# Sigmoid's table behind the last square root, and projections in the first two attention slots

## The chip, the cores and the metric

The kernel runs on one core of one Trainium2 chip. The metric is the device time of one execution in microseconds (us); the time of a kernel is the median over its runs. TensorE is called PE here, ScalarE ACT, VectorE DVE, GpSimd POOL and SyncE SP, as in the profile.

## The reference

One decoder layer over 1024 tokens of width 1024, in float32, with 16 learned meta tokens ahead of them:

```python
h = h + 0.5 * swiglu(rms_norm(h, ffn1_norm), ffn1_w_in, ffn1_w_out)
u = rms_norm(h, mix_norm) @ w_in                   # one combined projection
hq, hf, hi, hg, sq, sk, sv = split(u)
o_hg = hgrn2(hq, hf, hi, hg, lb, hgrn_out_norm)    # 4 heads, gated linear recurrence in chunks of 128
o_sb = stick_breaking(sq, sk, sv, q_norm, k_norm)  # 8 heads of 64, strictly causal
h = h + concat([o_hg, o_sb]) @ w_out
h = h + 0.5 * swiglu(rms_norm(h, ffn2_norm), ffn2_w_in, ffn2_w_out)
```

Stick breaking: `z = q.k / 8`, `A[t,s] = sigmoid(z_ts) * prod_{s<j<t} (1 - sigmoid(z_tj))`. The product over j is a running product along the keys of a row. In HGRN2 `f = lb + (1 - lb) * sigmoid(hf)`, `k = (1 - lb) * sigmoid(-hf)`, `q = silu(hq)`, and the gate is `silu(hg)`.

## The kernel before, in words

Every float32 product on PE is made of three products of rounded halves (`wh`, `wl`, `xh`, `xl`), the three lines L249 to L251 of `product`. The layer is staged: first feed-forward block (0 to about 735 us of the trace), the entry of the mixer, the attention, the four HGRN heads woven with the first half of the output product, the second half of that product, second feed-forward block. The change touches the entry and the attention.

**The entry.** `sb_project` makes keys, values and queries of two stick-breaking heads at a time (four pairs, p = 0 to 3), and two generators turn them: `sb_qk` transposes queries and keys, sums their squares into `sbs`, takes the square root of the sums on ACT (L1475), the reciprocal on DVE (L1476), scales on POOL (L1479), transposes back, and splits into halves `ohi` and `olo` that are stored. `weave` sets the order of the steps. ACT's functions come from tables: Sqrt has one, Sigmoid another, and an `ACT_TABLE_LOAD` stands where the table changes. Behind the four pairs the entry makes the first 16 pieces of the HGRN columns.

**HGRN columns.** `hgrn_fill` gives 96 pieces: 4 heads of columns v, f, q, g, each cut into two or four spans of tokens, each span into two pieces of 12 matmuls. A span is summed in one PSUM bank (`proj`); its second piece ends with the evacuation (`use`). For f these are two Sigmoids on ACT (L1141, L1142) and two DVE instructions, for q and g a Sigmoid (L1149) and a DVE product that reads the bank again (L1150). Results pass four staging tiles `st` and go to DRAM (`hg_v`, `hg_f`, `hg_k`, `hg_q`, `hg_g`). Column weights come by DMA into `raw`, are rounded by ACT (`wh`, L232) and subtracted by DVE (`wl`, L234).

**The attention.** `sb_jobs` yields 32 jobs: 8 heads, each with four pairs of query blocks (b0 = 0, 6, 2, 4). A job has scores (L1640 and L1641 on PE into one of two `z` buffers; L1642 `keep` and L1643 `sig`, two Sigmoids on ACT; L1646, the running product on DVE; L1653 on POOL), turns (transposes on PE, called `flip`, into one of two buffers; L1618 on ACT and L1619 on DVE make `wu` or, for the meta tokens, `wm`), and values (L1570 and L1572 on PE into `oacc`). `braid` sets the order on PE. It goes slot by slot; job i has its scores in slot i, its turns from slot i + 2 on, and its values from slot i + 3 on (`turn` = 2.0, `value` = 3.0). Each slot is owed 1.22 times its attention's time in projection pieces, which are spread evenly over the slot:

```python
owed += share * sum(t for _, t, _ in now)
while owed > 0:
    step = next(fill, None)
```

So slots 0 and 1, which hold scores alone, are owed little. In the attention only one bank serves the projections, since the other holds the constant `begin`; a new span therefore waits until ACT and DVE have emptied the bank. The other engines' rows follow the order in which the steps are written and the schedule of the recording layer.

**Behind the attention.** `hgrn_attend` loads a head's vT, KB, QA, F, KM and FM from DRAM (L1199, on SP's queue) and makes transposes of vT (`flip<-ident,vT`, L1495), the products within a chunk (`lvl`, L1235), and then seven levels (`lvl`, L1270, with the DVE products L1257 and the copies L1278). The loads of heads 0 to 2 are written behind the attention, as their tiles lie where its keys and queries lay. The projection pieces that `braid` has left over are woven with the first steps of the heads. Then follow the 64 steps of `first_half_of_o`, whose matmuls are called `wo`: they need `wh` and `wl` of the output weights (L222) and `oT`, the attention's result from DRAM (L2240), and all of these stand behind the head loads on SP's queue.

Of the kernel before, what the change touches and what calls it, by code (L numbers as in the profile page):

```python
# [15 lines left out]
AF = mybir.ActivationFunctionType  # L16
# [32 lines left out]
class Block:  # L49
# [1401 lines left out]
    def sb_qk(self, p, qT, kT, pool, mix, dst):  # L1451

        nc = self.nc
        ss, other = (
            pool.tile([P, 65], F32, tag=x, name=x, bufs=2) for x in ("sbs", "sbo")
        )  # L1460
        nat = pool.tile([P, 65, 32], F32, tag="nat", name="nat", bufs=2)
        rows = [(qT, 0, 0, 16), (qT, 512, 16, 16), (kT, 0, 32, 16), (kT, 512, 48, 17)]
        for src, c0, b0, nb in rows:
            y = nat[:, b0 : b0 + nb]
            nc.vector.transpose(y.rearrange("p b d -> p (b d)"), src[:, c0 : c0 + 32 * nb])
            sq = pool.tile([P, 17, 32], F32, tag="sq4", name="sq4", bufs=2)[:, :nb]
            nc.scalar.activation(sq, y, AF.Square)
            nc.vector.tensor_reduce(ss[:, b0 : b0 + nb], sq, mybir.AxisListType.X, ALU.add)
            yield 0, 1500
        for b in range(4):  # L1470
            nc.scalar.copy(
                other[32 * b : 32 * b + 32], ss[32 * (b ^ 1) : 32 * (b ^ 1) + 32]
            )
        nc.vector.tensor_add(ss, ss, other)
        nc.scalar.activation(ss, ss, AF.Sqrt, bias=self.eps, scale=1.0 / 64)  # L1475
        nc.vector.reciprocal(ss, ss)  # L1476
        for _, _, b0, nb in rows:
            y = nat[:, b0 : b0 + nb]
            nc.gpsimd.tensor_mul(  # L1479
                y, y, ss[:, b0 : b0 + nb].unsqueeze(2).broadcast_to([P, nb, 32])  # L1480
            )
        yield 0, 6000
        for src, c0, b0, nb in rows:
            t = src[:, c0 : c0 + 32 * nb]
            nc.vector.transpose(t, nat[:, b0 : b0 + nb].rearrange("p b d -> p (b d)"))
            n = min(32 * nb, (SEQ if src is qT else T) - c0)
            gain, to = (self.qg8, dst[0]) if src is qT else (self.kg, dst[1])
            with self.tc.issue_after(self.rounds[self.columns[-1]]) if p == 3 else ExitStack():
                self.put_split(to, p, slice(c0, c0 + n), t[:, :n], mix, gain)
            yield 0, 1500  # L1490
# [203 lines left out]
    def braid(self, jobs, fill, share, turn, value):  # L1694


        waiting = []
        owed = 0.0
        at = 0
        while True:  # L1700
            job = next(jobs, None)
            for lag, steps in zip((0.0, turn, value), job or ()):
                total, done = sum(t for t, _ in steps), 0.0
                for t, f in steps:
                    waiting.append((at + lag + (done + t / 2) / total, t, f))
                    done += t
            if not waiting:
                break
            now = [x for x in waiting if x[0] < at + 1]
            waiting = [x for x in waiting if x[0] >= at + 1]  # L1710
            owed += share * sum(t for _, t, _ in now)
            more = []
            while owed > 0:
                step = next(fill, None)
                if step is None:
                    break
                more.append(step)
                owed -= step[0]
            now += [(at + (i + 0.5) / len(more), t, f) for i, (t, f) in enumerate(more)]
            for _, _, f in sorted(now, key=lambda x: x[0]):  # L1720
                f()
            at += 1
# [669 lines left out]
```

## Time and profile before

| what | us |
| --- | --- |
| runs: median (lowest to highest of 3) | 1957.84 (1956.85 to 1957.93) |
| the profiled execution: its device time | 1959.65 |
| the profiled execution: its span | 1957.9 |
| PE busy / ACT busy / DVE busy / POOL busy | 1919.8 / 849.6 / 1390.4 / 450.5 |

The span is what the profile's windows and rows are counted from; the device time holds 1.75 us more around it. A row of the timeline gives start, length, engine, line, operation and, in brackets, how long the engine stood idle before it and who released it. PE is busy for 98% of the span, so the 38 us in which it is not are what a change of order can win or lose.

### The profile page before, as it was taken

Reading aid. Unit: us, or ns where it says so; the run is one execution under the profiler, and the core shown is the slowest. Engines: PE = TensorE matmul, PEld = TensorE weight load, DVE = VectorE, ACT = ScalarE, POOL = GpSimd, SP = SyncE. Lnnn points to the kernel's source line nnn. Section 1 sums busy time; section 2 is a strip of 40 time slices with the busy share of each in tenths; the row PEclk is TensorE's granted clock in tenths of the full one; section 3 lists DMA queues with packets and bytes.
Section 4 is the critical chain, followed back from the end, with each engine's and each line's share of the span. In section 5 each row is a group of like instructions: output and inputs, shape, how many; then the busy total and the mean of one; then the engine's idle time right before and its main releaser. Section 6 shows DMA issues by size and latency. Waiting matters only on the chain.

```text
span 1957.9 us, 30218 instructions
## 1 busy us (share of the span) xinstructions
PE 1919.8 (98%) x10607; PEld 1616.6 (83%) x10607; DVE 1390.4 (71%) x2184; ACT 849.6 (43%) x1711; POOL 450.5 (23%) x625
## 2 busy tenths in 40 slices
PE   7999999999999999999999999999999999999999
PEld 6888888788888888888898978887888888888887
DVE  7977877877678665467777766677567767766774
ACT  6523443334444544356666635433232332344443
POOL 3010100001000003133333332210544645530000
PEclk9999999999999999999999999999999999999999
DMA  7356887758965315865454177655634444469473
GB/s 213 93 165 170 253 272 243 233 203 291 375 221 188 127 54 144 193 170 148 128 148 121 57 253 225 161 208 183 198 115 140 128 131 121 132 243 318 154 231 113
DMA packets 381687, 355.54 MB, mean 182 GB/s; under 512 B 129040, under 2 KB 284560, under 8 KB 381536
## 3 DMA queue, kind: packets, MB, share of 16 engines
q1 hardware_dynamic: 359728, 288.98, 48.7%
q0 software_dynamic: 20768, 64.63, 9.5%
q8 instruction: 84, 1.38, 0.3%
q14 instruction: 67, 0.55, 0.1%
q10 hardware_dynamic: 1040, 0.00, 0.0%
HBM read 237.95 MB, written 115.57 MB: 181 GB/s over the span
## 4 chain that ended last, share of the span: by engine, by line
PE 89%; DVE 4%; DMA 3%; ACT 2%; issue 1%; POOL 1%; SPq 1%; DVEq 0%; ACTq 0%; POOLq 0%
PE o L732 21%; PE qb L450 18%; PE qa L450 12%; PE qc L450 12%; PE proj L249 5%; PE proj L251 4%; PE proj L250 4%; PE flip L1495 2%; PE wo L250 1%; PE wo L249 1%; PE wo L251 1%; PE mq L1001 1%; PE oacc L1572 1%; PE oacc L1570 1%; DMA oT<-oD 1%
## 5 line engine op out<-in xcount | busy, mean ns | idle before, releaser
L450 PE MATMUL qb<-T,wh 128*128 128x512 f32 x1056 | 344.6, 390 | 1.3 <-ACT T L309 0.8
L450 PEld LDWEIGHTS qb<-T,wh 128*128 128x128 f32 x1056 | 198.1, 188 | 46.4 <-issue 2.5
L450 PE MATMUL qa<-B,wh 128*128 128x512 f32 x696 | 226.7, 390 | 0.3 <-ACT B L835 0.2
L249 PE MATMUL proj<-xh,wh 128*128 128x512 f32 (+2 forms) x640 | 213.2, 333 | 2.6 <-ACT st L1142 1.3
L732 PE MATMUL o<-t,w 128*128 128x512 f32 x924 | 211.8, 390 | 0.7 <-DVE u L543 0.7
L251 PE MATMUL proj<-xl,wh 128*128 128x512 f32 (+2 forms) x640 | 210.2, 328 | 0.8 <-DVE xl L1957 0.8
L250 PE MATMUL proj<-xh,wl 128*128 128x512 f32 (+2 forms) x640 | 210.1, 328 | 0.0
L732 PE MATMUL o<-parts 128*128 128x512 f32 x924 | 209.6, 389 | 0.0
L450 PE MATMUL qb<-T,wl 128*128 128x512 f32 x528 | 205.5, 389 | 0.0
L732 PEld LDWEIGHTS o<-t,w 128*128 128x128 f32 x924 | 172.8, 188 | 37.8 <-ACT sgm L981 1.1
L732 PEld LDWEIGHTS o<-parts 128*128 128x128 f32 x924 | 173.5, 188 | 36.0
L362 DVE TENSOR_TENSOR wl<-s,wh 128x512 fp32r<-128x512 f32 x160 | 165.6, 1035 | 50.8 <-ACT wh L360 49.9
L360 ACT CAST wh<-s 128x512 fp32r<-128x512 f32 x160 | 99.2, 622 | 188.5 <-PE qb L450 141.1
L450 PEld LDWEIGHTS qa<-B,wh 128*128 128x128 f32 x696 | 130.5, 188 | 28.0 <-DVE B L836 0.5
L360 ACT CAST wh<-raw 128x512 fp32r<-128x512 f32 x120 | 74.4, 621 | 155.8 <-PE qc L450 111.4
L450 PE MATMUL qa<-B,wl 128*128 128x512 f32 x348 | 135.4, 389 | 0.0
L249 PEld LDWEIGHTS proj<-xh,wh 128*128 128x128 f32 x640 | 120.8, 189 | 15.0 <-ACT st L1142 2.2
L251 PEld LDWEIGHTS proj<-xl,wh 128*128 128x128 f32 x640 | 120.7, 189 | 12.3 <-DVE xl L1957 1.2
L250 PEld LDWEIGHTS proj<-xh,wl 128*128 128x128 f32 x640 | 120.8, 189 | 10.1
L450 PE MATMUL qc<-B,wh 128*128 128x512 f32 x352 | 115.1, 390 | 2.3 <-DVE u L543 2.3
L450 PE MATMUL qc<-T,wh 128*128 128x512 f32 x352 | 117.0, 394 | 0.0
L450 PEld LDWEIGHTS qb<-T,wl 128*128 128x128 f32 x528 | 99.1, 188 | 20.2
(393 smaller groups left out, 3819.4 us busy)
## 6 DMA issues: line engine op xcount, KB each, us to landing
raw<-in_ffn_w_in_dram SPq DMA_DIRECT2D x176, 256.0 KB, 4.0
raw<-in_ffn_w_out_dram SPq DMA_DIRECT2D x112, 256.0 KB, 4.5
w2in<-both SPq DMA_DIRECT2D x28, 512.0 KB, 3.4
raw<-in_w_in_dram SPq DMA_DIRECT2D x25, 512.0 KB, 5.2
ks<-kD SPq DMA_DIRECT2D x32, 260.0 KB, 4.8
wout<-both SPq DMA_DIRECT2D x16, 512.0 KB, 3.7
wh<-w2in SPq DMA_DIRECT2D x27, 256.0 KB, 3.1
wl<-w2in SPq DMA_DIRECT2D x27, 256.0 KB, 3.1
```

Of the source, the lines that this page charges most:

```text
L249: nc.tensor.matmul(ps, wh[:, s], xs, start=k == 0, stop=False)
L250: nc.tensor.matmul(ps, wl[:, s], xs, start=False, stop=False)
L251: nc.tensor.matmul(ps, wh[:, s], xl[:, k, c0 : c0 + n], start=False, stop=k == nk - 1)
L360: nc.scalar.copy(hi, src)
L362: self.block_lo = nc.vector.tensor_sub(lo, src, hi.bitcast(F32))
L450: nc.tensor.matmul(ps, a[:, k, :], b[:, k, :], start=start and k == 0 and i == 0, stop=k == 3 and i == 2, skip_group_check=True,)
L732: nc.tensor.matmul(banks[bank][m], y[:, m * P : (m + 1) * P], z, start=start and at == 0 and e == 0, stop=q == nq - 1 and e == 2, skip_gro ...
L1001: nc.tensor.matmul(ps[at : at + 32, :], self.xm[:, 4 * h + k, :], got[i, h][:, k, :], start=h == 0 and k == 0, stop=h == 1 and k == 3, til ...
L1495: self.nc.tensor.transpose(ps[:m, j, :], src[:, s0 : s0 + m], self.ident)
L1570: nc.tensor.matmul(o[:, c], vj, w[0], start=j == 0, stop=False, skip_group_check=True)
L1572: nc.tensor.matmul(o[:64, c], vj[:, :64], w[1], start=False, stop=end, skip_group_check=True)
```

## The change

In `sb_qk` of the last pair (p = 3) a Sigmoid of one column is issued right behind the square root; its result goes into `other` (`sbo` in the rows), which is no longer read. ACT thus loads Sigmoid's table there. In `braid`, slots below `turn` (0 and 1) are also owed the projections for the turns and values of their own jobs, which run in later slots.

```diff
-        nc.scalar.activation(ss, ss, AF.Sqrt, bias=self.eps, scale=1.0 / 64)
+        root = nc.scalar.activation(ss, ss, AF.Sqrt, bias=self.eps, scale=1.0 / 64)
+        if p == 3:
+            with self.tc.issue_after(root.ins):
+                nc.scalar.activation(other[:, :1], self.eps, AF.Sigmoid)
         nc.vector.reciprocal(ss, ss)
...
             owed += share * sum(t for _, t, _ in now)
+            if at < turn:
+                owed += share * sum(t for steps in job[1:] for t, _ in steps)
```

Lines behind the first edit move by 3, behind the second by 5. Counted from the planner's own numbers, slots 0 and 1 get 1 and 0 pieces before and 1 and 3 after; over the attention it is 74 pieces before, with 6 left for the first steps of the HGRN heads, and 76 after, with 4 left. The number of pieces, loads and stores is the same in all; one ACT instruction is added, and no table load.

On ACT, at the end of the entry (`+` and `-` as the difference shows them; `ohi` and `kT` belong to `sb_qk` of the last pair, `st` to the HGRN columns):

```order
 L1475 ACTIVATE sbs<-sbs,eps 128x65
+L1478 ACT_TABLE_LOAD
+L1478 ACTIVATE sbo<-eps 128x1
 L1416 ACTIVATE ohi<-qT,qg_82 128x512
 L1135 COPY st<-proj 128x256
...
 L1416 ACTIVATE ohi<-kT,kg 128x528
 L232 CAST wh<-raw 128x1024
-L1141 ACT_TABLE_LOAD
 L1141 ACTIVATE st<-proj 128x264
 L1142 ACTIVATE st<-proj 128x264
```

The load stood between the rounding of a weight and the first Sigmoid of a column f; it now stands behind the square root.

On PE, slot 1 of the attention before (the scores of the second job, in buffers `z`):

```order
L1640 MATMUL z<-ks,qs 128x456
L1641 MATMUL z<-ks,qs 128x456
...
L1640 MATMUL z<-ks,qs 128x344
L1641 MATMUL z<-ks,qs 128x344
L1640 MATMUL z<-ks,qs 128x348
L1641 MATMUL z<-ks,qs 128x348
```

and after, where each `proj` row of the three is one of four such threes in a piece:

```order
L1643 MATMUL z<-ks,qs 128x456
L1644 MATMUL z<-ks,qs 128x456
L249 MATMUL proj<-xh,wh 128x512
L250 MATMUL proj<-xh,wl 128x512
L251 MATMUL proj<-xl,wh 128x512
...
L1643 MATMUL z<-ks,qs 128x344
L1644 MATMUL z<-ks,qs 128x344
L1643 MATMUL z<-ks,qs 128x348
L1644 MATMUL z<-ks,qs 128x348
```

Three pieces have come between the scores of slot 1: behind the first 456 columns, behind the second, and behind the first 348. From there to the end of the attention the projections are ahead of where they stood by two to five pieces.

On PE, behind the attention before (four pieces of `proj` stand ahead of these rows; `proj` rows stand for the first of 12):

```order
L1495 MATMUL flip<-ident,vT 16x128
L1495 MATMUL flip<-ident,vT 128x128 x8
L249 MATMUL proj<-xh,wh 128x512
...
L1235 MATMUL lvl<-QA,KB 128x128 x8
L1495 MATMUL flip<-ident,vT 16x128
L1495 MATMUL flip<-ident,vT 128x128 x8
L249 MATMUL proj<-xh,wh 128x512
...
L1270 MATMUL lvl<-QA,KP 128x2x64 x4
L1235 MATMUL lvl<-QA,KB 128x128 x8
L1270 MATMUL lvl<-QA,KP 128x2x64 x4
```

and after, again behind four pieces:

```order
L1498 MATMUL flip<-ident,vT 16x128
L1498 MATMUL flip<-ident,vT 128x128 x8
L1498 MATMUL flip<-ident,vT 16x128
L1498 MATMUL flip<-ident,vT 128x128 x8
L1235 MATMUL lvl<-QA,KB 128x128 x16
L1270 MATMUL lvl<-QA,KP 128x2x64 x4
L249 MATMUL wo<-oT,wh 128x512
...
L1498 MATMUL flip<-ident,vT 16x128
L1498 MATMUL flip<-ident,vT 128x128 x8
L1270 MATMUL lvl<-QA,KP 128x2x64 x4
```

Two pieces are gone from here, and the first `wo` step now comes ahead of the third head's transposes and of two levels that preceded it. On SP the head loads, the last store and the loads of `wh`, `wl` and `oT` keep their order.

## The prediction

> **What bounds the kernel now.** I read the page first: engines, then the chain that ended last; then the windows of the attention (860 to 1140) and of the HGRN start (1140 to 1260).
>
> ```profile
> PE 1919.8 (98%) x10607; PEld 1616.6 (83%) x10607; DVE 1390.4 (71%) x2184; ACT 849.6 (43%) x1711; POOL 450.5 (23%) x625
> PE 89%; DVE 4%; DMA 3%; ACT 2%; issue 1%; POOL 1%; SPq 1%; DVEq 0%; ACTq 0%; POOLq 0%
> 860.00:1140.00 280.00, 270.99 (x1865) 244.43 (x1864) 205.11 (x356) 181.21 (x464) 98.86 (x141) 0.99 0.44 124
> 1140.00:1260.00 120.00, 113.02 (x736) 96.68 (x734) 82.05 (x152) 55.01 (x134) 37.62 (x73) 1.00 0.78 237
> ```
>
> PE bounds it. The change adds and removes no matmul, so its effect is PE's idle time and slow time, of which these two windows hold 9.0 and 7.0 us. The clock column (the third from the end: 0.99) says that some of the first was not idle but slow; finer windows find it:
>
> ```profile
> 867.00:868.00 1.00, 1.00 (x5) 0.95 (x5) 1.00 (x2) 1.00 (x5) 0.38 (x1) 0.63 1.00 207
> 868.00:869.00 1.00, 1.00 (x4) 0.71 (x4) 0.89 (x2) 0.74 (x3) 1.00 (x1) 0.50 1.07 237
> 869.00:870.00 1.00, 1.00 (x4) 0.81 (x3) 0.89 (x2) 0.00 (x0) 0.52 (x2) 0.50 0.94 184
> 870.00:871.00 1.00, 1.00 (x5) 0.76 (x4) 1.00 (x3) 0.00 (x0) 0.53 (x1) 0.66 1.21 230
> ```
>
> From 867.4 to 870.7 PE ran at half its clock: 0.37 + 0.5 + 0.5 + 0.34 = 1.7 us lost, behind four us of scattered scores.
>
> **Part 1, the table.** On ACT, then PE and SP:
>
> ```profile
> 844.47 0.72 ACT L1416 ACTIVATE ohi<-qT,qg 128x512 fp32r<-128x512 f32 x1 [2.58 <-DVE qT L1485]
> 850.22 1.03 ACT L232 CAST wh<-raw 128x1024 fp32r<-128x1024 f32 x1
> 851.27 1.28 ACT L1141 ACT_TABLE_LOAD   x1
> 852.56 0.39 ACT L1141 ACTIVATE st<-proj 128x264 f32<-128x264 f32 x1
> 854.72 0.39 ACT L1142 ACTIVATE st<-proj 128x264 f32<-128x264 f32 x1 [1.21 <-DMA hg_v<-st]
> 860.20 1.05 ACT L232 CAST wh<-raw 128x1024 fp32r<-128x1024 f32 x1 [3.14 <-DMA raw<-in_w_in_dram]
> 861.86 0.30 ACT L1643 ACTIVATE sig<-z 128x144 f32<-128x144 f32 x1
> 853.28 0.39 PE L249 MATMUL proj<-xh,wh 128*128 128x256 f32 x1 [1.31 <-ACT st L1142]
> 855.29 0.46 SPq L227 DMA_DIRECT2D raw<-in_w_in_dram  x1
> ```
>
> New place: the load (1.28) and a Sigmoid of one column (under the 0.30 of 144 columns) fall into the 2.58 us in which ACT waits for DVE behind the square root; DVE's reciprocal needs only the root. Price 0; without that cover the `ohi` stores would be 1.6 us late. Old place: ACT's chain cast, load, Sigmoid, Sigmoid held the bank for which PE waited 1.31. Now that wait is about 0. But the gain does not last. The second span's L1142 waits for a store (854.72) that the change does not touch, so the fourth span starts at 855.16 instead of 856.15: 1.0 left. Then ACT rounds a weight at 860.20 whose DMA was issued at 855.29, on a queue whose order and releases are the same; two Sigmoids and the first scores' `keep` and `sig` stand behind it, and the score of 456 columns needs the buffer that `sig` empties at 862.16. PE comes there 1 us earlier and waits 1 us longer. Of 1.3 us about 0.1 is left.
>
> The Trainium skill ("ScalarE: Activation LUTs", What ACT_TABLE_LOAD costs) gives 1283 ns for a load and 1380 more for a drain. The trace has the first and not the second (cast over at 851.25, load at 851.27, Sigmoid at 852.56); by the page the load would stick out of the 2.58 by some 0.3 us.
>
> **Part 2, slots 0 and 1.** PE's waits here, the span of a projection piece (859.22 to 862.04: 2.8 us), and DVE:
>
> ```profile
> 859.22 0.44 PE L249 MATMUL proj<-xh,wh 128*128 128x512 f32 x1
> 862.04 0.29 PE L1640 MATMUL z<-ks,qs 128*128 128x272 f32 x1
> 863.23 0.48 PE L1640 MATMUL z<-ks,qs 128*128 128x456 f32 x1 [0.33 <-ACT sig L1643]
> 864.11 0.43 PE L1640 MATMUL z<-ks,qs 128*128 128x344 f32 x1 [0.21 <-ACT sig L1643]
> 865.00 0.43 PE L1640 MATMUL z<-ks,qs 128*128 128x348 f32 x1 [0.31 <-ACT sig L1643]
> 866.08 0.43 PE L1640 MATMUL z<-ks,qs 128*128 128x348 f32 x1 [0.49 <-ACT sig L1643]
> 873.25 0.42 PE L1640 MATMUL z<-ks,qs 128*128 128x328 f32 x1 [0.55 <-ACT sig L1643]
> 864.14 6.18 DVE L1646 TENSOR_TENSOR_SCAN keep<-keep,begin 128x144 f32<-128x144 f32 x7
> 872.66 0.69 DVE L1150 TENSOR_TENSOR st<-st,proj 128x512 f32<-128x512 f32 x1 [0.95 <-ACT st L1149]
> ```
>
> Before: 1.9 us of idle, 1.7 of half clock. After, worked forward: score 456 at 862.2, piece 2 to 865.4, score 456 to 865.8. Piece 3 opens a new span, and the one bank is emptied by L1149 and then L1150, which stands on DVE behind the scans of 144, 272 and 457 columns (873 of the 2448 of the seven: 2.2 us from 864.14, to 866.3) and takes 0.69: piece 3 at 867.0, a wait of 1.1. Piece 3, two scores, piece 4: to 873.2. Now five scores and the first transposes stand with no projection at all. ACT frees a `z` buffer every 0.9 us as before (0.6 us wait), the meta transpose needs a buffer that DVE empties behind four scans, a split and L1150 (1.4), the next four transposes another (0.6). The score of 328 columns starts at 876.7; before it started at 873.25 with two pieces fewer (5.6 us), which makes 2.1 gained, 1.6 behind the last wait. But PE is busy there from 873.2 to 878 for some 45% of the time, as it was from 863 to 867, and that was followed by half clock: if it comes again, 1.7 goes. I take that: part 1 and the slots together 0.0, bounds -1.7 and +0.7.
>
> The rest of the attention has some 6.5 us of waits between 884 and 1135, dealt anew as pieces move by two to five places: 0, bounds 1.5 either way (a quarter). At its end, slot 33 has one piece instead of two between transposes that share two buffers: +0.4, bounds 0 and 0.8.
>
> **Part 3, behind the attention.** Two pieces (5.6 us) now lie in the attention, so it ends 5.6 us later, and head loads start then.
>
> ```profile
> 1135.35 0.39 PE L249 MATMUL proj<-xh,wh 128*128 128x512 f32 x1
> 1146.46 1.30 PE L1495 MATMUL flip<-ident,vT 128*16 128x128 f32 x9
> 1150.37 1.95 PE L1235 MATMUL lvl<-QA,KB 128*128 128x128 f32 x16
> 1161.80 0.66 PE L1495 MATMUL flip<-ident,vT 128*128 128x128 f32 x4 [0.68 <-ACT vr L1223]
> 1163.23 0.48 PE L249 MATMUL wo<-oT,wh 128*128 128x512 f32 x1
> 1166.99 0.50 PE L251 MATMUL wo<-oT,wh 128*128 128x512 f32 x1 [1.45 <-DMA oT<-oD]
> 1167.65 0.50 PE L249 MATMUL wo<-oT,wh 128*128 128x512 f32 x1 [0.16 <-DMA oT<-oD]
> 1138.21 0.37 SPq L1199 DMA_DIRECT2D vT<-hg_v  x1
> 1151.49 0.32 SPq L1199 DMA_DIRECT2D FM<-hg_f  x1
> 1157.01 0.32 SPq L222 DMA_DIRECT2D wh<-wout  x1
> SPq L222 <- PE proj L251: 4.1, 1, 4.1
> F<-hg_f SPq DMA_DIRECT2D x3, 512.0 KB, 7.6
> oT<-oD SPq DMA_DIRECT2D x8, 256.0 KB, 7.8
> ```
>
> Let E be the attention's end, 1135.35 before. SP issues the 18 head loads from E + 2.9 to E + 16.1; before, it then waited 4.1 for PE's last projection, and `wh` went out at E + 21.7. The first `wo` ran at E + 27.9 without a wait, and PE had 1.6 us of waits right behind it. After, the last projection is done at E' + 11.1 (four pieces, as 1135.35 to 1146.46), so `wh`, `wl` and the first two `oT` go out from E' + 17 to 19. The third F (about 13.6) lands at 21.2; behind it 1 MB is to come, 3.1 us at the rate of the head loads (estimated: 3 x 2.07 MB between E + 2.9 and E + 21.2), so 24.3; by the 7.8 of `oT`'s row it is 19 + 7.8 = 26.8. I take 24.7, nearer to the rate, since the bytes are what it waits for. With E' = E + 5.6 the first `wo` comes at E + 30.3, 2.4 later than before. PE has by then only 11.1 + 2 x 1.05 (transposes, 1146.46 to the next piece) + 2 x 1.8 (products, 16 rows) + 0.9 (a level, 8 rows) = 17.7 us of work in E' + 24.7: it stands 7 us idle, and one group of transposes and two levels (2.85) that were done before are still to do. Against this, the 1.6 of waits go; 0.5 comes for the transposes' own buffers (0.68 in the row of 1161.80). 2.4 + 2.85 - 1.6 + 0.5 = +4.2; bounds +2.1 (24.3, no 0.5, and the levels left over fill 1.2 of the 4 us of waits that the window has later) and +5.6 (everything as late as the loads).
>
> Then the clock: 5 us and more of standing still is more than the scattered four that cost 1.7 before; I put +1.0, for PE may wait for `oT` again meanwhile, bounds 0 and 1.7. The Trainium skill ("TensorE: Matmul & The Clock Gate", Part 1) has the clock halved after an idle window of about 3.4 us and restored after as long a busy one. The trace agrees on 3.3 us of half clock, but it came behind waits of at most 0.49 each, and not behind the 1.45 and 0.16 of 1166 to 1168. By that rule alone the price here is half of 3.4, 1.7, and the sum 0.7 higher.
>
> **Sum.** 0.0 + 0 + 0.4 + 4.2 + 1.0 = +5.6 on a span of 1957.9 us. The profiled execution's 1959.65 is 1.8 over the median of the runs shown; the difference is put on the median: 1963.4.
>
> **Rivals.**
> - *The slots pay.* If PE's clock stays up behind slot 1 (three pieces now stand among the scores, and the half clock's window may fall otherwise), 1.6 to 2.1 is won there; with a head-load price at its low bound (+2.1) and the clock up there as well, the result is +0.5 to +2: about 1959, no change that counts. For it: the row of 1166.99, after which the clock stood (the window's 1.00). The Trainium skill's clock rule, cited above, would have it so in slot 1 too, where no wait is 3.4 us long. Against: the 7 us that PE now has nothing to do.
> - *Faster.* The loads behind the attention come in time: `oT` in PE's reach by E' + 18, when its 17.7 us of work are done. Then only the slots count: -2, with luck in the 6.5 us -4: 1954. It decides at E' + 20. Against: SP cannot have issued the third head's loads before E' + 16, and the loads before `oT` are the same.
> - *Lanes bound.* DVE is the heads' bottleneck once levels run, and it starts as late as the head loads: the whole 5.6 stays, with the clock +7.5 to +9: 1966.
> - *The table load is not hidden any more, or never was:* worth at most 1.3 either way, inside each of these.
>
> **How the numbers follow.** A measurement of this kernel tells about 0.2% (3.9 us) from no change. The forecast (+4 to +7) has 0.45, lanes bound 0.17, the slots pay 0.31, faster 0.07. Of the forecast's, a few land under 3.9, of the slots' some above: slower 0.60, same 0.33, faster 0.07. Range: 1957.5 (a gain in slots and waits of 2.5 against the low bound) to 1967.5.
>
> **What would show it.** The table load behind 841.9 and no PE wait at L1142's release near 852, but one of about 1 us at the first 456-column score; a wait of 1 us for L1150 in slot 1; half clock once between 874 and 882; the last projection ahead of the first vT transposes; PE idle by 5 us or more ahead of the first `wo`, ended by a DMA, and half clock behind it. I am wrong if `oT` lands by E' + 20, if the idle time ahead of `wo` is under 3 us, or if the rest of the attention's waits change by more than 2.

## The result, and the profile after

| | before | after |
| --- | --- | --- |
| device time, median of 4 runs each (lowest to highest) | 1957.67 (1956.85 to 1957.93) | 1976.26 (1976.05 to 1978.24) |
| the profiled execution: device time / span | 1959.65 / 1957.9 | 1976.05 / 1974.3 |

The ratio is 1.0095 (95% interval 1.008 to 1.0111): 18.6 us slower. Forecast were 1963.4 and at most 1967.5. The direction was right, the size was not.

The page of the kernel after (engines, then the chain that ended last):

```profile
PE 1922.3 (97%) x10607; PEld 1619.5 (82%) x10607; DVE 1392.9 (71%) x2184; ACT 849.3 (43%) x1712; POOL 448.8 (23%) x625
PE 85%; DMA 5%; DVE 5%; ACT 2%; issue 2%; SPq 1%; POOL 0%; DVEq 0%; ACTq 0%; POOLq 0%
```

The spans differ by 16.4. PE's busy time grew by 2.5 with the same matmuls; its idle time grew from 38.1 to 52.0, by 13.9. DMA has gone from 3% to 5% of the chain: a load is waited for that was not before. Of the 16.4, 1.4 have arisen by 452 us, in the first feed-forward block, which the change does not touch (0.6 of idle and 0.8 of busy time); 15.0 are left for the change, 13.3 of them idle and 1.7 busy. The same two windows as before (PE's busy time is the second number, its granted clock the third from the end):

```profile
860.00:1140.00 280.00, 266.24 (x1836) 240.51 (x1835) 199.84 (x321) 178.24 (x457) 97.48 (x139) 0.99 0.43 122
1140.00:1260.00 120.00, 105.82 (x670) 91.64 (x668) 82.62 (x170) 51.15 (x121) 36.70 (x74) 0.96 0.75 227
```

PE is busy for 4.75 us less in the attention's window and for 7.2 us less behind it. The places, in order of time. The entry on ACT:

```profile
843.29 1.28 ACT L1478 ACT_TABLE_LOAD   x1
844.58 0.20 ACT L1478 ACTIVATE sbo<-eps 128x1 f32<-128x1 f32 x1
845.85 0.73 ACT L1416 ACTIVATE ohi<-qT,qg 128x512 fp32r<-128x512 f32 x1 [1.06 <-DVE qT L1488]
861.02 1.05 ACT L232 CAST wh<-raw 128x1024 fp32r<-128x1024 f32 x1 [3.01 <-DMA raw<-in_w_in_dram]
```

The load and the Sigmoid lie inside ACT's wait for DVE, of which 1.06 is left. The rounding of the next weight (L232) starts at 861.02, against 860.20 before; without the first block's 1.4 that is 0.6 earlier. Slots 0 to 2 on PE:

```profile
867.90 0.50 PE L249 MATMUL proj<-xh,wh 128*128 128x512 f32 x1 [0.99 <-DVE st L1150]
876.91 0.39 PE L1643 MATMUL z<-ks,qs 128*128 128x264 f32 x1 [1.52 <-ACT sig L1646]
878.60 0.50 PE L1552 MATMUL flip<-ident,sig 128*16 128x128 f32 x2 [1.17 <-DVE wu L1622]
```

Three waits of 1.0 to 1.5 us stand where five of 0.2 to 0.55 were. The transposes of the attention from 885 us to its end, grouped by shape (the last part of a row is PE's idle time ahead of the group), before:

```profile
L1495 PE MATMUL flip<-ident,sig 128*128 128x128 f32 x267 | 44.2, 274 | 5.2 <-DVE wu L1619 3.2 <-DVE wm L1619 1.8
L1549 PE MATMUL flip<-ident,sig 128*16 128x128 f32 x60 | 11.4, 272 | 0.2 <-DVE wu L1619 0.2
```

and after:

```profile
L1498 PE MATMUL flip<-ident,sig 128*128 128x128 f32 x278 | 46.0, 275 | 9.1 <-DVE wu L1622 7.7 <-DVE wm L1622 1.2
L1552 PE MATMUL flip<-ident,sig 128*16 128x128 f32 x62 | 11.8, 272 | 1.6 <-DVE wu L1622 1.5
```

The same kind of transposes waits 10.7 us instead of 5.4 for a buffer that DVE has not emptied. And behind the attention, which now ends at E' = 1145.85; PE first, then SP's queue:

```profile
1159.74 1.30 PE L1498 MATMUL flip<-ident,vT 128*16 128x128 f32 x9 [1.47 <-DMA vT<-hg_v]
1171.56 0.76 PE L249 MATMUL wo<-oT,wh 128*128 128x512 f32 x1 [6.03 <-DMA oT<-oD]
1199.29 0.56 PE L249 MATMUL wo<-oT,wh 128*128 128x512 f32 x1 [1.86 <-DMA wh<-wout]
1234.66 1.30 PE L1498 MATMUL flip<-ident,vT 128*16 128x128 f32 x9 [2.27 <-DMA vT<-hg_v]
1290.01 0.63 PE L1354 MATMUL onp<-ident,vT 128*128 128x128 f32 x4 [2.27 <-DVE vT L1348]
1149.15 0.37 SPq L1199 DMA_DIRECT2D vT<-hg_v  x1
1163.60 0.32 SPq L1199 DMA_DIRECT2D FM<-hg_f  x1
1164.49 0.38 SPq L222 DMA_DIRECT2D wh<-wout  x1
1166.23 3.81 SPq L2245 DMA_DIRECT2D oT<-oD  x5
1227.65 0.32 SPq L1199 DMA_DIRECT2D vT<-hg_v  x1
```

PE stands idle for 7.5 us ahead of the first `wo` step, ended by a DMA, and then three more times for about 2 us each: for output weights, for the fourth head's vT (issued behind ten `wh` loads), and for the last head's DVE work. The clock there:

```profile
1160.00:1170.00 10.00, 5.53 (x49) 5.16 (x46) 8.11 (x11) 2.60 (x4) 8.44 (x28) 0.94 1.04 379
1170.00:1180.00 10.00, 8.44 (x46) 7.56 (x46) 5.76 (x8) 3.07 (x5) 4.53 (x14) 0.72 0.82 258
1200.00:1201.00 1.00, 1.00 (x3) 0.61 (x4) 0.00 (x0) 0.03 (x1) 0.00 (x0) 0.50 1.04 207
```

In the trace it is halved from 1168.9 for 6.83 us and from 1199.6 for 3.41 us; before, it was not halved in this stretch.

### The profile page after: what moved, and what is told of

The parts are those of the page before. It is cut to its first block, busy times and chain, and to the rows that moved or that the text cites. A ratio compares the mean times of both kernels' runs of the same rounds, so it can differ in the third digit from the quotient of the medians.

```text
span 1974.3 us, 30221 instructions
## 1 busy us (share of the span) xinstructions
PE 1922.3 (97%) x10607; PEld 1619.5 (82%) x10607; DVE 1392.9 (71%) x2184; ACT 849.3 (43%) x1712; POOL 448.8 (23%) x625
## 4 chain that ended last, share of the span: by engine, by line
PE 85%; DMA 5%; DVE 5%; ACT 2%; issue 2%; SPq 1%; POOL 0%; DVEq 0%; ACTq 0%; POOLq 0%
PE o L732 21%; PE qb L450 18%; PE qa L450 12%; PE qc L450 12%; PE proj L249 4%; PE proj L251 4%; PE proj L250 3%; PE flip L1498 1%; PE wo L250 1%; PE wo L251 1%; PE wo L249 1%; DMA wl<-wout 1%; PE mq L1001 1%; PE oacc L1575 1%; PE oacc L1573 1%
```

## The experiments

Each was timed beside the kernel before, whose median was 1958.5 to 1958.8 there. The table has what all of them have in common: the projection pieces in slots 0 and 1, in the attention and behind it, the time, and PE's waits, added up from the brackets of its timeline (0.15 us and longer) from 858 to 885 us, from there to the attention's last matmul, and on to 1500 us. The profiled executions are 0.6 to 3.1 us later than the one of the kernel before by the end of the first feed-forward block, which no edit touches; so small differences are read from the medians and from the waits, not from single spans.

| kernel | pieces in slots 0, 1; attention; behind | median us | ratio to before (95%) | waits: slots / rest / behind |
| --- | --- | --- | --- | --- |
| before | 1, 0; 74; 6 | 1957.7 | | 2.3 / 6.5 / 8.0 |
| after | 1, 3; 76; 4 | 1976.3 | 1.0095 (1.008 to 1.0111) | 3.8 / 10.6 / 16.9 |
| e1 table only | 1, 0; 74; 6 | 1959.3 | 1.0006 (0.9997 to 1.0015) | 2.4 / 6.9 / 8.0 |
| e2 slots only | 1, 3; 76; 4 | 1977.7 | 1.0098 (1.0082 to 1.0113) | 3.2 / 10.4 / 17.0 |
| e3 | 1, 3; 74; 6 | 1964.1 | 1.003 (1.0018 to 1.0043) | 5.1 / 10.0 / 7.6 |
| e4 | 1, 0; 76; 4 | 1971.8 | 1.0067 (1.0053 to 1.0081) | 2.1 / 4.8 / 16.8 |
| e5 warm | 1, 3; 76; 4 | 1979.1 | 1.0096 (1.0079 to 1.0113) | 4.5 / 10.4 / 16.4 |
| e6 `wo` later | 1, 3; 76; 4 | 1973.3 | 1.008 (1.0064 to 1.0095) | 4.6 / 10.4 / 14.7 |
| e7 | 1, 2; 72; 8 | 1987.9 | 1.0146 (1.013 to 1.0162) | 2.4 / 7.2 / 26.9 |
| e8 | 1, 0; 72; 8 | 1992.7 | 1.0169 (1.0152 to 1.0186) | 2.6 / 8.9 / 26.0 |
| e9 idle pieces | 1, 3; 76; 4 + 2 idle | 1969.7 | 1.0057 (1.0044 to 1.0071) | 4.6 / 10.5 / 6.2 |
| e10 idle pieces | 1, 0; 76; 4 + 2 idle | 1962.8 | 1.002 (1.0011 to 1.0029) | 1.8 / 4.8 / 6.3 |
| e11 | 1, 1; 74; 6 | 1963.7 | 1.0024 (1.0015 to 1.0033) | 4.3 / 9.4 / 7.1 |
| e12 | 1, 2; 74; 6 | 1962.0 | 1.0018 (1.0009 to 1.0027) | 1.9 / 9.8 / 8.2 |
| e13 before, DVE work left out | 1, 0; 74; 6 | 1955.8 | 0.9987 (0.9976 to 0.9998) | 1.7 / 5.2 / 5.6 |
| e14 e12, DVE work left out | 1, 2; 74; 6 | 1955.1 | 0.9981 (0.9969 to 0.9992) | 1.9 / 6.5 / 6.9 |
| e15 after, DVE work left out | 1, 3; 76; 4 | 1973.8 | 1.0077 (1.0048 to 1.0106) | 2.4 / 10.1 / 16.5 |

**Which part costs: e1 to e4.** e1 is the first edit alone, e2 the second alone. e3 is the changed kernel with a share of 1.17 (`islice(columns, 76), 1.17`), e4 the kernel before with 1.25.

> Only the first edit: Sigmoid's table behind the last square root, braid as before. Theory A (the loss is in the two pieces moved from behind the attention into it): the table edit wins PE's wait of 1.31 us near 853 and gives it back at the first 456-column score, where ACT's weight rounding waits for its DMA: -0.3 to 0 us. Rival B (the table edit has part in the loss, by a drain or by shifting ACT and DVE): +1 to +4 us. Rival C (the win stays): -1.3 us.

> Only the second edit: slots 0 and 1 are owed more, the table load where it was. Theory A: the whole loss, +17 to +19 us over before, with the 6 us wait for oT ahead of the first wo matmul and half clock behind it. Rival B: +13 to +16, the rest belongs to the table edit.

> Both edits, but share 1.17 instead of 1.22: slots 0 and 1 get 1 and 3 pieces as in the changed kernel, the attention takes 74 pieces as before, so 6 are left behind it. Theory A: what happens behind the attention is as before (first wo without a long wait, one half-clock spell in all, near the first slots); the waits in the attention stay: +2 to +5 us over before. Rival D (the crowded first slots are the loss): +14 to +18 us. Rival E (the slots pay once the pieces behind the attention are kept): -4 to 0 us.

> The kernel before with share 1.25 instead of 1.22: slots 0 and 1 as before, but the attention takes 76 pieces and 4 are left behind it, with the order behind the attention of the changed kernel. Theory A: +10 to +15 us over before, with a wait of 5 to 7 us for oT ahead of the first wo, and half clock behind it. Rival D (the crowded first slots are the loss): 0 to +3 us.

The table's new place shows no effect: the 0.8 of e1 is inside its interval. The whole loss is the second edit's (e2). It has two halves: with the new slots and the old count behind the attention +5.6 (e3, a little over theory A's 2 to 5), with the old slots and two pieces fewer there +13.3 (e4, within A's 10 to 15). Together 18.9, against 18.6 and, for e2, 19.2. In e4 the waits behind the attention are those of the changed kernel (its profiled run was the fastest of four, 1966.9):

```profile
1163.34 0.77 PE L249 MATMUL wo<-oT,wh 128*128 128x512 f32 x1 [5.39 <-DMA oT<-oD]
1191.27 0.50 PE L249 MATMUL wo<-oT,wh 128*128 128x512 f32 x1 [2.82 <-DMA wh<-wout]
1225.54 1.30 PE L1495 MATMUL flip<-ident,vT 128*16 128x128 f32 x9 [2.40 <-DMA vT<-hg_v]
```

**Is it the clock: e5.**

```diff
                         yield 4000.0
+                        warm = self.pproj.tile([P, 512], F32, tag="proj", name="warm")
+                        for _ in range(40):
+                            nc.tensor.transpose(warm[:, :P], self.ident, self.ident)
                         plan = [(m, half) for half in range(2) for m in range(KT)]
```

> The changed kernel with 40 transposes of the identity put on PE ahead of the first wo step; nothing reads them. They fill 5.1 us (0.127 each, from the vT transposes) of the 6.03 us in which PE waits for oT, so its clock should stay up. Theory A (the missing pieces leave a wait for oT, and the clock is a loss of its own on top of it): the spell of half clock at 1168.9 goes; 4.2 us of it lay on running matmuls and cost 2.1, so 1.0 to 2.5 less than the changed kernel, about 1974.5; the wait itself stays. Rival B (the heads on DVE start as late as their loads and bound what follows, so PE's speed here is worth nothing): 0 within 1 us, and the later waits for DVE and DMA grow by what the clock gives.

```profile
1166.39 4.53 PE L2260 MATMUL warm<-ident 128*128 128x128 f32 x40
1173.52 0.52 PE L249 MATMUL wo<-oT,wh 128*128 128x512 f32 x1 [2.61 <-DMA oT<-oD]
1201.29 0.80 PE L249 MATMUL wo<-oT,wh 128*128 128x512 f32 x1 [3.07 <-DMA wh<-wout]
1237.80 1.59 PE L1498 MATMUL flip<-ident,vT 128*16 128x128 f32 x9 [3.73 <-DMA vT<-hg_v]
1174.00:1177.00 3.00, 3.00 (x14) 2.63 (x13) 0.28 (x1) 0.73 (x2) 1.72 (x11) 0.50 0.85 245
```

A miss for theory A. Useless work in the wait gains nothing: 1979.1 against 1976.3, with intervals that overlap (the profiled run was the slowest of four, 1981.9). It did not even keep the clock up: the window's 0.50 is one of three spells of 3.41 us behind the attention, as much in all as in the changed kernel (10.2). What the price of the clock by itself is, this run does not say. It does show that the waits of 1199 and 1234 grow (1.86 to 3.07, 2.27 to 3.73) where the first one shrinks: in this order it is data that sets the pace up to there.

**Order without cover: e6.** The planner's cost of the loads is raised from 4000 to 9000 (`yield 9000.0`).

> The changed kernel with 9000 instead of 4000 as the planner's cost of the loads ahead of the first wo step: the third head's transposes and two levels stand ahead of that step again, as before the change, and the fourth head's vT is loaded one pair of weights earlier. Theory A (what is lost is PE's time in the wait, with work still to do behind it): 2.85 us of work and the waits for DVE inside it move into the 7.5 us without work, the wait for oT falls from 6.0 to between 1 and 3.5, the half clock there goes or halves, and the waits of 1.9 (weights) and 2.3 (vT) later are smaller; 4 to 8 less than the changed kernel, 1968 to 1972. Rival B (the lanes bound): the time lost stays, only under other names; within 2 us of 1976.

3.0 us better than the changed kernel, or 4.1 when each is counted from the kernel before that was timed beside it; the two intervals overlap. Either way it lies at or under the lower end of theory A's 4 to 8 and above B's 2, so it decides for neither. The wait for `oT` is gone, but the third head's transposes and the fourth's wait instead (the profiled run was the slowest of four, 1979.3):

```profile
1170.24 1.12 PE L1498 MATMUL flip<-ident,vT 128*128 128x128 f32 x4 [3.21 <-ACT vr L1223]
1229.45 1.11 PE L1498 MATMUL flip<-ident,vT 128*128 128x128 f32 x4 [3.14 <-DVE vm L1220]
```

The old order alone thus wins back 3 to 4 of the 18.6: it has little to put into the time of the loads.

**More pieces behind: e7 and e8.** The changed kernel with a share of 1.12, and the kernel before with 1.17.

> Both edits, with a share of 1.12: slots 0 and 1 get 1 and 2 pieces, the attention 72, and 8 are left behind it (74 and 6 before, 76 and 4 after the change). Theory A (each piece left behind the attention covers 2.8 us of the head loads as long as PE waits there): the two more pieces find only the 1.6 us of waits for oT that the kernel before has, and the new slots lose less with 2 pieces than with 3: 1 to 4 better than 74 pieces with the new slots, so 1960 to 1963.5. Rival C (the loss in the slots and re-dealt waits, +5.6 there, is not tied to the count): 1964 within 1.5.

> The kernel before with a share of 1.17: the old slots, 72 pieces in the attention and 8 left behind it. Theory A: the waits behind the attention (1.45 and 0.16 for oT) go, other waits of the attention are dealt anew by up to 1.5 either way: 0 to 3 less than before, about 1956.5. Rival D (the pieces behind the attention delay the heads, which DVE bounds, by 5.6 for two more): 3 or more slower, 1961 to 1964.

Every theory missed: +29 and +34. The loss is not a slope of 2.8 us a piece. With eight pieces left the planner puts nearly all levels of three heads between them, and the first `wo` 45 us later. Rows of e8 (the levels from 1140 to 1200 as a group, the first `wo`, and a later one):

```profile
L1270 PE MATMUL lvl<-QA,KP 128*128 128x128 f32 x160 | 24.9, 315 | 8.7 <-ACT KP L1264 8.6
1208.62 0.47 PE L249 MATMUL wo<-oT,wh 128*128 128x512 f32 x1 [2.58 <-DMA oT<-oD]
1281.35 0.47 PE L249 MATMUL wo<-oT,wh 128*128 128x512 f32 x1 [1.97 <-DMA wh<-wout]
```

The levels, with nothing between them, wait for ACT, and when they are used up the output product stands alone with its weights' loads (1.97 at 1281.35). Of e8's span, 33.7 us longer than before, the waits behind the attention make 18.0 and PE's longer busy time 12.0; the clock was halved there four times, for 20.5 us in all. Four pieces left and eight are both far worse than six; five and seven were not tried.

**Cover and order together: e9 and e10.** Two idle pieces in `rest`, in the changed kernel and in e4:

```diff
+                        spare = self.proj_bank(512)
+                        def idle_piece():
+                            for i in range(22):
+                                nc.tensor.transpose(
+                                    spare[:, P * (i % 4) : P * (i % 4 + 1)], self.ident, self.ident)
-                        left = list(columns)
+                        left = [(12 * (512 * 0.42 + 13), idle_piece)] * 2 + list(columns)
```

> The changed kernel with two pieces' worth of transposes of the identity (44, read by nobody, about 5.6 us of PE) ahead of its four last projection pieces behind the attention, and counted by the planner as pieces, so that the order of heads and output product is that of the kernel before again. It has more work and computes nothing more. Theory G (the two moved pieces were free where they lay, since they covered the head loads and kept the order of the heads' steps; moved into the attention they cost their own 5.6 us, and the wait and the order behind cost the rest): the waits behind the attention fall from 16.9 us to about 8, the half clock there goes, and the 5.6 are paid: about 5 less than the changed kernel, 1969 to 1972, in spite of the added work. Rival B (the heads on DVE start as late as the attention ends, and bound all that follows): the added work lies in time that PE waits for anyway; 1976 within 1.5. Rival H (PE bounds throughout): 5.6 more, 1982.

> The same two idle pieces in the kernel with the old slots and 76 pieces in the attention, which measured 1971.8. Theory G: the kernel before plus 5.6 us of work, 1964 within 1.5, so about 8 less than without the idle pieces. Rival B: 1971.8 within 1.5. Rival H: 1977.

Theory G holds in both. 44 transposes that nobody reads make the changed kernel 6.5 us faster and e4 9.1 us faster. Rows of e9 (PE, then the window behind the attention):

```profile
1148.97 4.96 PE L2211 MATMUL proj<-ident 128*128 128x128 f32 x44
1174.69 0.66 PE L1498 MATMUL flip<-ident,vT 128*128 128x128 f32 x4 [0.68 <-ACT vr L1223]
1176.20 0.47 PE L249 MATMUL wo<-oT,wh 128*128 128x512 f32 x1
1140.00:1260.00 120.00, 113.66 (x755) 97.69 (x754) 84.34 (x175) 55.01 (x131) 38.92 (x74) 1.00 0.75 229
```

The first `wo` comes 27.2 us behind the attention's end (1148.97), without a wait, as in the kernel before (27.9); no half clock there, and the waits behind the attention are 6.2 instead of 16.9. B and H fall: the heads start no earlier than in the changed kernel and the end is earlier. The 10.7 us of waits that go are paid for with the 5.0 us of the transposes. Cover without the old order was not run, so how the gain divides between the two is known only as far as e6 shows it.

**Which deal: e11 and e12.** What slots 0 and 1 are owed for their later steps is multiplied by 0.5 (share 1.18) and by 0.6 (share 1.17).

> Both edits, with what slots 0 and 1 are owed for their later steps halved and a share of 1.18: they get 1 and 1 pieces (1 and 0 before, 1 and 3 after the change), and 74 lie in the attention as before, so that nothing changes behind it. Theory C (what the new slots cost at 74 pieces, +5.6, comes of the third and second piece in slot 1: the wait for L1150, the late weight and the later transposes' waits): 0 to 2 more than the kernel before. Rival F (the kernel before lies at a good deal of its waits, and any other deal costs): 3 to 6 more.

> Both edits, with 0.6 of what slots 0 and 1 are owed for their later steps and a share of 1.17: they get 1 and 2 pieces, and 74 lie in the attention as before. Theory C: between slots of 1 and 1 and slots of 1 and 3, 0.5 to 3.5 more than the kernel before; the waits up to 885 us about 2.4 as with 1 and 2 pieces and a share of 1.12, against 5.1 with 3 in slot 1. Rival F: 3 to 6 more, as with 1 and 1.

+5.0 and +3.3: theory C falls by e11, since one piece in slot 1 costs about as much as three (+5.6 in e3); e12 alone would fit C as well. F holds for 74 pieces, where every new deal tried lost 3 to 6. It does not hold for any deal: with the old slots and 76 pieces (e4, e10) the waits in the rest of the attention are 4.8, less than the 6.5 before. The transposes' groups of e12, from 885 us to the attention's end, wait 9.5 us, against 5.4 before:

```profile
L1498 PE MATMUL flip<-ident,sig 128*128 128x128 f32 x273 | 45.1, 274 | 9.0 <-DVE wu L1622 7.6 <-DVE wm L1622 1.2
L1552 PE MATMUL flip<-ident,sig 128*16 128x128 f32 x62 | 11.8, 272 | 0.5 <-DVE wu L1622 0.4
```

One of these waits, and what DVE and POOL did ahead of it:

```profile
936.60 0.30 PE L1498 MATMUL flip<-ident,sig 128*128 128x128 f32 x1 [1.60 <-DVE wu L1622]
931.81 1.90 DVE L1146 TENSOR_SCALAR st<-st,lbc 128x264 f32<-128x264 f32 x1
933.63 0.68 DVE L1622 TENSOR_TENSOR wu<-flip,wu 128x512 fp32r<-128x512 f32 x1
934.23 1.90 DVE L1649 TENSOR_TENSOR_SCAN keep<-keep,begin 128x345 f32<-128x345 f32 x2
936.05 0.40 DVE L1622 TENSOR_TENSOR wu<-flip,wu 128x256 fp32r<-128x256 f32 x1
931.76 1.80 POOL L1656 TENSOR_TENSOR sig<-sig,keep 128x912 f32<-128x912 f32 x1 [2.43 <-DVE keep L1649]
```

The `wu` of 936.05 ended this wait. A projection's evacuation (L1146) stood ahead of it on DVE and took 1.90; behind that came another `wu` and two scans.

**Is it DVE's work for the projections: e13 to e15.** In `use` these lines are left out, from the kernel before, from e12 and from the changed kernel:

```diff
-                nc.vector.tensor_scalar(
-                    t, t, self.lbc[:, h : h + 1], self.lb[:, h : h + 1], ALU.mult, ALU.add
-                )
-                nc.vector.tensor_scalar_mul(k, k, self.lbc[:, h : h + 1])
...
-                nc.vector.tensor_mul(t, t, ps)
```

> The kernel before without DVE's work on the HGRN columns f, q and g (L1143, L1146 and L1150 are left out, so the forget gates, keys, queries and gates that are stored are bare sigmoids): 48 DVE instructions fewer, 36 of them in the attention; PE's order and the loads stay. Theory J (the transposes of the attention wait for wu because DVE has just taken an instruction of a projection ahead of it): the transposes' waits between 885 us and the attention's end fall from 5.4 us to 2 to 4. Rival K (the waits come of the place of the pieces on PE, whatever DVE does for them): 5 to 6.

> The same left out of the kernel with slots of 1 and 2 pieces and 74 in the attention. Theory J: the transposes' waits fall from 9.5 us to 3 to 6, and the difference to the kernel before without that work is under 2 us (4.1 with it). Rival K: 8.5 to 10, the difference stays.

> The same left out of the changed kernel. Theory J: the transposes' waits in the attention fall from 10.7 us to 3 to 7, of the difference of 5.3 to the kernel before under 2.5 is left; the wait of 0.99 for L1150 in slot 1 goes; the waits behind the attention stay at about 17. Rival K: 9.5 to 11.

The transposes' rows of e14:

```profile
L1493 PE MATMUL flip<-ident,sig 128*128 128x128 f32 x267 | 44.1, 274 | 5.2 <-DVE wu L1617 3.7 <-DVE wm L1617 1.2
L1547 PE MATMUL flip<-ident,sig 128*16 128x128 f32 x60 | 11.4, 272 | 1.6 <-DVE wu L1617 1.6
```

A divided answer. In e14 the waits fall from 9.5 to 6.8, not quite to theory J's 3 to 6, and the loss of that deal is gone, as J had it: 0.6 less than e13, where e12 lay 3.3 above the kernel before. In e13 they stay (5.4 to 5.2), as K had it, and in e15 too (10.7 to 10.3). So DVE's instructions for the projections make the loss of the deal with slots of 1 and 2. In the changed kernel they don't (e15 has two runs; its wait for the bank in slot 1 fell from 0.99 to 0.32, the later ones stayed). The place of its pieces on PE and the weights' subtraction (L234), which was left in, are what remains. The trace of e15 shows something of both: its longest wait in the attention (1.59 us, at 992.4) has an L234 of 2.35 us just ahead of its `wu`, and the one of 1.21 at 1081.2 has no L234 among the five DVE instructions ahead of it. No run separates the two.

## Why the prediction was wrong

Point by point, from the profile after, with PE's waits as in the table:

| step | predicted | found |
| --- | --- | --- |
| table and slots together | 0.0 | +0.4: of the 1.31 of L1142 0.20 is left, 1.5 more between 858 and 885 |
| rest of the attention and its end | +0.4 | +4.1 |
| behind the attention, waits | +4.2 | +8.9 |
| clock there | +1.0 | at most +1.7: PE's longer busy time without the first block's 0.8 |
| sum | +5.6 | +15.1; the spans without the first block's 1.4 say 15.0 |

**What held.** The table load lay in the wait named for it, and what it gained did not last. In e1 it was lost where the prediction put it: the load of the next weight went out no earlier, and the first 456-column score waited 1.80 where it had waited 0.33. In the changed kernel that score waited only 0.16, so this sign did not come; there the gain went in the three waits of the slots. The wait for L1150 in slot 1 was 0.99 (predicted 1.1), the half clock came at 878.7 (874 to 882), although one reason given for it was misread: before, PE was busy for 2.75 of the 4 us from 863 to 867, 69% and not 45%; the 264-column score waited longer (1.52 for 0.6). Behind the attention the last projection stood ahead of the first vT transposes, `wh` went out at E' + 18.6 (17), the first `wo` ran at E' + 25.7 (24.7), and PE's idle time ahead of it was 7.5 (7). The growth of the waits up to that point, 7.5 less the 3.0 that were there before, is 4.5, the 4.2 of the sum. The Trainium skill ("ScalarE: Activation LUTs", What ACT_TABLE_LOAD costs) counts a drain on top of the load; the trace after shows none either, for the next instruction followed at 844.58, 10 ns behind the load.

**Step one that failed: "the rest of the attention ... dealt anew ...: 0, bounds 1.5 either way".** It is 4.1, in transposes that wait for DVE; the prediction's own sign of being wrong, a change of more than 2 there, came. The bound, a quarter of the 6.5, had no row behind it. What makes DVE late is shown for the slots of 1 and 2 (e14) and open for the changed kernel's own (e15). A deal is not a random draw around the one that stands there: of the deals with 72 to 76 pieces that were run, the new slots gave 7.2 to 10.6 and the old ones 4.8 to 8.9. e3, e11 and e12 show it, with the slots, apart from what comes behind the attention (+5.6, +5.0, +3.3).

**Step two: part 3, "everything as late as the loads" as the upper bound, 5.6.** The term took it that once `oT` was there the rest would run as before, with the later waits at 4. They became 8.1: 1.86 for weights, 2.27 for the fourth head's vT, 2.27 for the last head's end and small ones. The levels and the transposes put behind the first `wo` came late, the fourth head's loads were issued later (E' + 81.8 for its vT, against E + 77.0 before); why the weights came late at 1199 was not followed further. e9 shows the whole of it: with cover and order put back, 10.7 us of waits vanish. The rival "lanes bound" came nearer with its 1966, by a wrong cause: DVE does not bound the heads by their late start, or e9 would have gained nothing.

**Step three: the clock, 1.0.** There were two spells, not one; the second began 0.3 us behind the wait of 1.86 for weights. What they cost by themselves no run shows; PE's busy time bounds it by 1.7.

The two failed terms are of the same kind: both took a change of order as neutral outside the place looked at.

## What to carry to other kernels

Work that lies in the shadow of loads is free there and costs its full length elsewhere: before moving it, sum what PE has left for the time until the loads land, and then follow the order on to the next two or three loads, since a late start comes back at each. An order that a planner has made from costs is no smooth function of them: two pieces more or fewer cost 13 and 34 us here, and 44 useless transposes in the right place gained 6.5 to 9. A count that is to be changed is best tried alone, with everything behind it kept in its order.

## What the runs showed of the hardware

- DVE instructions of the same shape differ by a factor of five: L1146 on 264 columns takes about 0.35 us in seven of its eight instructions in e12, and 1.90 in one, where a POOL instruction ran from 931.76 for 1.80; DVE's ended 0.15 behind it. In the changed kernel L234 took 2.34 us beside a POOL instruction of 1.34; other rows of it have 1.23. The Trainium skill ("SBUF — State Buffer", Who interferes with whom) says that DVE and GpSimd share a port pair, and that where an instruction of each needs it (on DVE one with two SBUF inputs, as L234, or one in a two-port mode) the order of issue decides which of the two is blocked. These rows fit; whether L1146 runs in such a mode no run here shows.
- The half clock came in spells of 3.41 or 6.83 us and no other length, but for the one that each trace ends in. It came within 6 us of idle time (after), behind waits of half a microsecond in slot 1 (before), and behind 2.61 us in e5 with 4.5 us of transposes ahead of them. The Trainium skill ("TensorE: Matmul & The Clock Gate", Part 1) ties it to an idle window of about 3.4 us; the length agrees, but here it also came where no wait was longer than half a microsecond. In the slots the same program, as far as PE's order goes, had a spell of 3.41 (before), one of 6.83 (e1) or none (e4).
